# A background sum stepped at every fourth stop of a recurrence in both layers, instead of at every second stop in the first

## The chip, the cores and the metric

The kernel runs on one core of one Trainium2 chip. The metric is device time of one execution in microseconds (us). TensorE is PE in the profile (its weight loads are PEld), VectorE is DVE, ScalarE is ACT, GpSimd is POOL, and SP issues most of the DMAs.

## The reference, cut to what matters

Two transformer-like blocks, each of two layers, run one after the other on a sequence of 512 x 1024 in float32. The first block has four branches per layer, of which one (RWKV-7) is a recurrence over time. The second block scales and shifts its activations by vectors that depend on nothing but two small inputs and a large matrix:

```python
def first_block(x, ...):
    for l in range(2):
        h = x @ w_in[l]                      # 1024 x 10016
        # y_rwkv: a scan over 512 steps, 8 heads, state 64 x 64
        # y_mla, y_conv, y_mem: two attentions and a convolution
        merged = sum(sigmoid(h_merge[n] + b_gate[n]) * (y[n] @ w_o_branch[l][n]) for n in range(4))
        x = layer_norm(ALPHA * x + merged @ w_out[l])
    return x

def second_block(x, c, ctx, c_ctx, w_ada, ...):
    for i in range(2):
        mod_x = silu(c) @ w_ada[i] + b_ada[i]        # w_ada[i] is 1024 x 6144
        mod_c = silu(c_ctx) @ w_ada[i] + b_ada[i]
        hx = rms_norm(x) * (1 + sc1) + sh1           # pieces of mod_x
        ...                                          # attention, pooling, Fourier mix, feed-forward
```

`mod_x` and `mod_c` for `i = 0` do not depend on the first block, so their sums can be made at any time before the second block starts.

## The kernel before, in words

Every weight matrix is streamed from HBM in pieces of 512 KB. `wload` (lines 224 to 250) gets a piece into a tile `wst` by a DMA from SP, ACT rounds it into `wh`, DVE subtracts to get the rest `wl` (`split`, line 208), and `mm3` (line 203) makes each product with three matmuls. There are two buffers of `wst` and four of `wh` and of `wl` (`self.wb = (2, 4)`). A `wst` buffer is free again once `wl` is made.

The modulation sums are a generator, `ada(l)` (lines 1320 to 1347). It takes `w_ada` in 24 column blocks of 256 and each block in two halves of 512 rows. A half is one DMA of 512 KB into a `wst` tile of the same two buffers (line 1331); then DVE multiplies and adds its four row groups into `aacc`, once for `c` and once for `c_ctx`: eight DVE instructions per half, and only after the last of them is the buffer free. After both halves come two transposes into `atr` (line 1344) and a reduction into `adared` (line 1345). For `l = 0` the generator yields five times per block, 120 times in all. `tick2` (line 170) advances it by one yield, if there is one left.

The recurrence is `rwkv` (lines 522 to 869). It works by 64-step chunks: `prep` and `operands` make the operands of a head pair, `triangles` the 64 x 64 triangular matrices (through small DMAs `tri`, `BL`, `stk` of SP), `substitute` and `doubling` invert them, `chain` carries the state from chunk to chunk through short PE, DVE and ACT steps (`rbd`, `ubd`, `sbd`), and `close` normalises. Wherever these generators yield, `turns` calls `spot`: a stop. At a stop `drip` advances the filler of large matmuls (the merges of the three other branches, and gates), and `tick2` may advance the modulation sums. There are 248 stops per layer (5 of `prep`, 5 of `triangles`, 8, 12 of `doubling`, seven rounds of 29, and 15). `spots` is counted anew in each layer.

Before, `tick2` is called at each odd stop: 124 calls in the first layer, enough for all 120 yields, so the generator is exhausted there and the calls of the second layer do nothing. After the second layer's recurrence `while self.bg2: self.tick2()` (line 1297) would finish what is left. The sums of the second block's second layer (`ada(1)`) run later, in the feed-forward, and are not touched.

The order in which instructions stand on each engine is made when the kernel is built, by a scheduler that goes by priorities and by when it thinks an engine will be free; every engine then works through its own list in order. Weights have a higher priority than what stands around them (`high_priority` in `wload`).

Of the kernel before, what the change touches and what calls it, by code (L numbers as in the profile page):

```python
# [127 lines left out]
class K:  # L128
# [393 lines left out]
    def rwkv(self, l, st):  # L522
# [286 lines left out]
        spots = [0]  # L809

        def spot(w):

            self.drip(w)
            spots[0] += 1
            if spots[0] % 2:
                self.tick2()

        def turns(w, main, *side):

            for _ in main:  # L820
                spot(w)
                for t in side:
                    next(t, None)
            for t in side:
                for _ in t:
                    spot(w)
# [16 lines left out]
        for _ in prep(0):  # L843
            spot(0.5)
# [1174 lines left out]
```

## Time and profile before

| | |
|---|---|
| median of 3 runs | 3273.27 us (3270.59 to 3274.57) |
| the profiled execution | 3272.34 us |
| its span, first to last instruction | 3270.3 us |
| PE busy, share of the span | 3126.8 us, 96% |
| DVE busy | 2300.7 us, 70% |
| ACT busy | 1276.8 us, 39% |
| mean granted TensorE clock | 0.984 |

Times in the views are from the start of the span. The recurrence of the first layer lies at about 327 to 857 us, that of the second at 1239 to 1705 us, and the feed-forward of the second block's first layer at about 2080 to 2640 us. A clock of 1.00 in a view is 2.4 GHz throughout; the other level is 1.2 GHz.

### The profile page before, as it was taken

The page shows a single profiled execution, that of the slowest core. Times are in us where ns is not written, and L with a number is a line of the kernel's source. Part 1 is how long each engine was busy: PE and PEld are TensorE (multiplying, and loading weights), DVE is VectorE, ACT ScalarE, POOL GpSimd, SP SyncE. Part 2 cuts the span into 40 slices and gives each one's busy share as a digit, 9 for nine tenths or more (in the row PEclk, how much of TensorE's full clock was granted, in tenths as well). Part 3 has the DMA queues.
Part 4 walks back from the last instruction along what each step waited for, and adds up shares of the span by engine and source line. Part 5 has one row for each costly group of instructions (what it writes and reads, how often), then busy time and mean ns, then how long its engine had stood idle before and what let it go on. Part 6 is the DMA issues. An engine that isn't in the chain of part 4 may idle for free.

```text
span 3270.3 us, 44267 instructions
## 1 busy us (share of the span) xinstructions
PE 3126.8 (96%) x16694; PEld 2610.3 (80%) x16694; DVE 2300.7 (70%) x4916; ACT 1276.8 (39%) x2332; POOL 85.3 (3%) x176
## 2 busy tenths in 40 slices
PE   8999999899999999999999799989999999999999
PEld 7877777687898778888889776878888887688887
DVE  8978888888769886666658887875464468863342
ACT  4445333333344464444434556312121234732221
POOL 0001000000000000000000000000000000000000
PEclk9999999999999999999999899999999999999999
DMA  5322334334453223223234212344343232123332
GB/s 176 89 63 66 110 107 114 100 102 116 146 149 84 58 59 86 63 71 82 63 112 116 76 51 79 100 121 128 103 135 91 86 112 73 42 85 97 97 98 88
DMA packets 438661, 310.07 MB, mean 95 GB/s; under 512 B 69024, under 2 KB 430544, under 8 KB 438448
## 3 DMA queue, kind: packets, MB, share of 16 engines
q1 hardware_dynamic: 431392, 292.60, 31.0%
q0 software_dynamic: 7056, 14.65, 1.8%
q8 instruction: 132, 2.16, 0.3%
q14 instruction: 81, 0.66, 0.1%
HBM read 295.13 MB, written 7.34 MB: 92 GB/s over the span
## 4 chain that ended last, share of the span: by engine, by line
PE 49%; DVE 8%; DMA 3%; ACT 3%; issue 1%; SPq 0%; ACTq 0%; POOL 0%; DVEq 0%
PE ps_mm L197 40%; PE ps_o L197 2%; PE ps_tp L197 2%; DMA wst<-in_w_gate_up_dram 2%; DVE wl L186 2%; PE ps_aux L197 1%; PE ps_sc L197 1%; ACT wh L209 1%; DVE aacc L194 1%; DMA wst<-in_w_in_dram 1%; PE ps_mx L197 1%; PE ps_yb L197 1%; DVE n2t L194 0%; DVE z L186 0%; DMA wst<-in_w_ada_dram 0%
## 5 line engine op out<-in xcount | busy, mean ns | idle before, releaser
L209 ACT CAST wh<-wst 128x1024 fp32r<-128x1024 f32 (+3 forms) x453 | 458.5, 1013 | 1035.5 <-PE ps_mm L197 563.9
L186 DVE TENSOR_TENSOR wl<-wst,wh 128x1024 fp32r<-128x1024 f32 (+3 forms) x453 | 532.4, 1175 | 341.3 <-ACT wh L209 337.3
L197 PE MATMUL ps_mm<-xh,wh 128*128 128x512 f32 (+1 forms) x1200 | 499.7, 417 | 20.8 <-ACT wh L209 16.8
L197 PE MATMUL ps_mm<-xh,wl 128*128 128x512 f32 (+1 forms) x1200 | 482.2, 402 | 1.9 <-DVE wl L186 1.8
L197 PE MATMUL ps_mm<-xl,wh 128*128 128x512 f32 (+1 forms) x1200 | 482.4, 402 | 0.0
L197 PE MATMUL ps_mm<-h8h,wh 128*128 128x512 f32 (+1 forms) x928 | 360.6, 390 | 14.0 <-ACT wh L209 12.4
L197 PE MATMUL ps_mm<-h8h,wl 128*128 128x512 f32 (+1 forms) x928 | 357.2, 386 | 3.4 <-DVE wl L186 3.4
L197 PE MATMUL ps_mm<-h8l,wh 128*128 128x512 f32 (+1 forms) x928 | 358.8, 387 | 0.1
L197 PEld LDWEIGHTS ps_mm<-xh,wh 128*128 128x128 f32 (+1 forms) x1200 | 228.8, 191 | 65.6 <-ACT wh L209 20.4
L197 PEld LDWEIGHTS ps_mm<-xh,wl 128*128 128x128 f32 (+1 forms) x1200 | 227.5, 190 | 51.9 <-DVE wl L186 6.4
L194 DVE SCALAR_TENSOR_TENSOR aacc<-wst,silc,aacc 128x256 f32<-128x256 f32 x560 | 250.7, 477 | 19.7 <-DMA wst<-in_w_ada_dram 15.8
L197 PEld LDWEIGHTS ps_mm<-xl,wh 128*128 128x128 f32 (+1 forms) x1200 | 228.7, 191 | 37.7 <-issue 0.2
L197 PEld LDWEIGHTS ps_mm<-h8h,wl 128*128 128x128 f32 x928 | 176.3, 190 | 41.5 <-DVE wl L186 6.1
L197 PEld LDWEIGHTS ps_mm<-h8h,wh 128*128 128x128 f32 x928 | 176.6, 191 | 36.8 <-ACT wh L209 14.4
L197 PEld LDWEIGHTS ps_mm<-h8l,wh 128*128 128x128 f32 x928 | 176.8, 191 | 20.7 <-DVE h8l L194 0.4
L197 PE MATMUL ps_mm<-fh,wl 128*128 128x512 f32 (+1 forms) x528 | 186.8, 354 | 2.1 <-DVE wl L186 2.1
L197 PE MATMUL ps_mm<-fl,wh 128*128 128x512 f32 (+1 forms) x528 | 187.6, 355 | 0.0
L197 PE MATMUL ps_mm<-fh,wh 128*128 128x512 f32 (+1 forms) x528 | 187.3, 355 | 0.0
L194 DVE SCALAR_TENSOR_TENSOR ft<-ft,ps_mm 128x512 f32<-128x512 f32 (+1 forms) x134 | 76.6, 586 | 138.5 <-PE ps_mm L197 80.6
L194 DVE SCALAR_TENSOR_TENSOR cacc<-ch,vec,cacc 128x512 f32<-128x512 f32 x240 | 168.7, 746 | 2.3 <-ACT cacc L183 1.8
L197 PE MATMUL ps_mm<-hch,wl 128*128 128x256 f32 x448 | 126.7, 284 | 1.8 <-DVE wl L186 1.8
L197 PE MATMUL ps_mm<-hcl,wh 128*128 128x256 f32 x448 | 126.5, 284 | 0.7 <-DVE hcl L194 0.6
(549 smaller groups left out, 6413.9 us busy)
## 6 DMA issues: line engine op xcount, KB each, us to landing
wst<-in_w_in_dram SPq DMA_DIRECT2D x188, 512.0 KB, 3.9
wst<-in_w_ada_dram SPq DMA_DIRECT2D x96, 512.0 KB, 3.7
wst<-in_w_gate_up_dram SPq DMA_DIRECT2D x88, 512.0 KB, 4.0
wst<-in_w_out_dram SPq DMA_DIRECT2D x40, 512.0 KB, 3.5
wst<-in_w_down_dram SPq DMA_DIRECT2D x36, 512.0 KB, 3.5
wst<-in_w_o_branch_dram SPq DMA_DIRECT2D x32, 512.0 KB, 3.5
wst<-in_xattn_w_mem_kv_dram SPq DMA_DIRECT2D x16, 512.0 KB, 3.5
wst<-in_w_down_dram SPq DMA_DIRECT2D x20, 384.0 KB, 3.1
```

The lines of the kernel that those rows point to most:

```text
L186: return self.nc.vector.tensor_tensor(out=out, in0=a, in1=b, op=op)
L194: return self.nc.vector.scalar_tensor_tensor(out=out, in0=a, scalar=s, in1=b, op0=op0, op1=op1)
L197: self.nc.tensor.matmul(out, lhsT=l, rhs=r, start=start, stop=stop)
L209: self.nc.scalar.copy(out=h, in_=src)
```

## The change

The condition in `spot` is different, and nothing else:

```diff
             self.drip(w)
             spots[0] += 1
-            if spots[0] % 2:
+            if spots[0] % 4 == 1:
                 self.tick2()
```

Now 62 of the 248 stops of a layer advance the sums. The generator gets 62 of its 120 yields in the first layer and the other 58 in the second. In halves of `w_ada`, which are DMAs: before, 48 in the first layer; now 25 in the first and 23 in the second.

What stands on SP in the first layer, between the load of the fourth triangle (`BL<-tri_85`) and that of the fifth (`BL<-tri_84`). Before:

```order
L656 DMA BL<-tri_85 64x8x8
L1331 DMA wst<-in_w_ada_dram 128x4x256
L235 DMA wst<-in_w_in_dram 128x8x128 x2
L1331 DMA wst<-in_w_ada_dram 128x4x256
L695 DMA tri_87<-sub_3147 64x8x8
L698 DMA stk<-tri_87 32x4x32 x4
L235 DMA wst<-in_w_o_branch_dram 128x4x256
L235 DMA wst<-in_w_in_dram 128x4x256 x2
L1331 DMA wst<-in_w_ada_dram 128x4x256 x4
L235 DMA wst<-in_w_o_branch_dram 128x4x256
L654 DMA tri_84<-AB 64x4x64 x2
L656 DMA BL<-tri_84 64x8x8
```

And now, at the same place on SP:

```order
L656 DMA BL<-tri_85 64x8x8
L235 DMA wst<-in_w_in_dram 128x8x128 x2
L695 DMA tri_87<-sub_3147 64x8x8
L698 DMA stk<-tri_87 32x4x32 x4
L1331 DMA wst<-in_w_ada_dram 128x4x256
L235 DMA wst<-in_w_o_branch_dram 128x4x256
L235 DMA wst<-in_w_in_dram 128x4x256 x2
L1331 DMA wst<-in_w_ada_dram 128x4x256 x2
L235 DMA wst<-in_w_o_branch_dram 128x4x256
L654 DMA tri_84<-AB 64x4x64 x2
L235 DMA wst<-in_w_in_dram 128x4x256
L656 DMA BL<-tri_84 64x8x8
```

Six loads of `w_ada` stood here, four of them in a row; now there are three, at most two in a row. Six pieces of weights stood here before, and seven now.

The same in the second layer, from its first triangle (`BL<-tri_84`) to its second (`BL<-tri_85`). Before:

```order
L656 DMA BL<-tri_84 64x8x8
L235 DMA wst<-in_w_o_branch_dram 128x4x256
L235 DMA wst<-in_w_in_dram 128x4x256
L695 DMA tri_86<-sub_11633 64x8x8
L235 DMA wst<-in_w_in_dram 128x4x256
L698 DMA stk<-tri_86 32x4x32 x4
L235 DMA wst<-in_w_in_dram 128x8x128 x2
L654 DMA tri_85<-AB 64x4x64 x2
L235 DMA wst<-in_w_in_dram 128x8x128
L656 DMA BL<-tri_85 64x8x8
```

And now:

```order
L656 DMA BL<-tri_84 64x8x8
L1331 DMA wst<-in_w_ada_dram 128x4x256
L235 DMA wst<-in_w_o_branch_dram 128x4x256
L695 DMA tri_86<-sub_11344 64x8x8
L698 DMA stk<-tri_86 32x4x32 x4
L235 DMA wst<-in_w_in_dram 128x4x256 x2
L1331 DMA wst<-in_w_ada_dram 128x4x256
L235 DMA wst<-in_w_in_dram 128x8x128
L654 DMA tri_85<-AB 64x4x64 x2
L656 DMA BL<-tri_85 64x8x8
```

Two loads of `w_ada` stand here now, where there was none, each with weights before and behind it. Outside the two recurrences the lists of DVE and SP read alike before and after.

## Rows read from the trace of the kernel before

**Rows 1.** The page: the span in 40 slices of 82 us
```profile
DVE  8978888888769886666658887875464468863342
...
PEclk9999999999999999999999899999999999999999
```

**Rows 2.** Where the recurrences begin (wlal) and end (yf of each layer)
```profile
L194 DVE SCALAR_TENSOR_TENSOR wlal<-ps_mm,om,mx x2: 743/743/743, 326.2 to 1239.1; 128x511 f32<-128x511 f32 x2
...
L194 DVE SCALAR_TENSOR_TENSOR yf<-yc,g x4: 684/685/692, 510.1 to 856.9; 128x512 f32<-128x512 f32 x4
...
L194 DVE SCALAR_TENSOR_TENSOR yf<-yc,g x4: 648/650/692, 1406.1 to 1704.3; 128x512 f32<-128x512 f32 x4
```

**Rows 3.** Busy time by stretch: the two recurrences; the next-to-last figures are clock, DMA share
```profile
core 0: us, PE busy (x) PEld busy (x) DVE busy (x) ACT busy (x) POOL busy (x), PEclk, DMA share, GB/s
327.00:857.00 530.00, 487.75 (x2479) 399.79 (x2478) 449.27 (x1227) 192.96 (x416) 3.16 (x6) 0.95 0.38 110
1239.00:1705.00 466.00, 463.75 (x2503) 384.51 (x2502) 285.86 (x779) 191.65 (x416) 5.58 (x11) 1.00 0.28 74
```

**Rows 4.** What PE waited for, 327 to 857 us: us, times, longest
```profile
PE ps_mm L197 <- ACT wh L209: 16.8, 13, 4.0
PE ps_aux L197 <- ACT ubd L745: 5.6, 6, 3.4
PE ps_aux L197 <- ACT rbd L745: 5.1, 6, 3.0
PE ps_tp L197 <- DVE stk L732: 3.9, 3, 3.1
PE ps_tp L197 <- DVE X L186: 2.3, 1, 2.3
```

**Rows 5.** Instructions on wst, 327 to 857 us (ns min/median/max), and their waits
```profile
L194 DVE SCALAR_TENSOR_TENSOR aacc<-wst,silc,aacc x330: 433/476/487, 335.2 to 832.8; 128x256 f32<-128x256 f32 x165
L209 ACT CAST wh<-wst x60: 1033/1047/1057, 329.4 to 856.4; 128x1024 fp32r<-128x1024 f32 x60
L186 DVE TENSOR_TENSOR wl<-wst,wh x59: 1194/1224/1227, 330.5 to 854.3; 128x1024 fp32r<-128x1024 f32 x59
L1331 SPq DMA_DIRECT2D wst<-in_w_ada_dram x47: 367/368/597, 331.7 to 824.0; - x47
...
  PE ps_mm L197: 28.0, 7
...
  ACT wh L209: 62.0, 33
...
DMA to landing us min/median/max: 3.3/3.7/5.3
```

**Rows 6.** The same, 1239 to 1705 us
```profile
  PE ps_mm L197: 105.6, 38
...
  ACT wh L209: 4.3, 3
```

**Rows 7.** The feed-forward and a stretch of full DVE: columns as in rows 3
```profile
2300.00:2600.00 300.00, 298.10 (x1691) 259.20 (x1690) 150.05 (x266) 59.02 (x88) 0.00 (x0) 1.00 0.36 108
...
1000.00:1050.00 50.00, 49.95 (x248) 41.40 (x247) 49.23 (x83) 24.37 (x56) 0.55 (x1) 1.00 0.31 85
```

**Rows 8.** Loads of w_ada, 2300 to 2600 us: ns min/median/max, first and last
```profile
L1331 SPq DMA_DIRECT2D wst<-in_w_ada_dram x24: 367/368/368, 2330.5 to 2529.6; - x24
```

**Rows 9.** Two gaps of PE in order of time: 504 to 512 and 591 to 594 us
```profile
504.15 1.05 ACT L209 CAST wh<-wst 128x1024 fp32r<-128x1024 f32 x1 [4.86 <-DMA wst<-in_w_o_branch_dram]
...
512.09 0.79 PE L197 MATMUL ps_mm<-xh,wh 128*128 128x512 f32 x1 [3.98 <-ACT wh L209]
...
593.17 0.47 DVE L194 SCALAR_TENSOR_TENSOR aacc<-wst,silc,aacc 128x256 f32<-128x256 f32 x1
593.57 0.21 DVE L744 COPY rbd<-ps_yb 64x64 f32<-64x64 f32 x1
...
594.12 0.49 PE L197 MATMUL ps_aux<-rbd,AB 128*128 128x128 f32 x2 [3.02 <-ACT rbd L745]
```

## The prediction, made before the changed kernel had run

> **What bounds the kernel now.** I read first the busy shares. PE is busy 96% of the span by the table above. DVE by slices of 82 us [rows 1] is at 7 or 8 tenths between 330 and 860 us (fifth to eleventh slice), and at 5 or 6 tenths between 1240 and 1700 us (sixteenth to twenty-first). The dips of the clock are hardly readable there, since a slice is long; they show below.
>
> Then I found the two recurrences by their first and last instructions [rows 2]: 326.2 to 857.6 us in the first layer (856.9 plus 0.7 for the last `yf`), 1239.1 to 1705.0 us in the second. They do the same work, and one is 531 us and the other 466 us long. The reader is to see in the two stretches side by side [rows 3] that PE has 2479 and 2503 records in them (some records are missing from a trace), but is idle for 42 us of 530 in the first and for 2 us of 466 in the second; and that the same matmuls are busy for 488 us in the first and 464 us in the second, where the granted clock is 0.95 against 1.00. So the first layer loses 65 us: 40 to gaps of PE, 24 to the clock that falls to 1.2 GHz in and behind the gaps. What the first layer has and the second has not is the modulation sums: DVE is busy 449 us there and 286 us here, 163 us more.
>
> Third I read what PE waits for in the first recurrence [rows 4]. Two kinds come out at the same size: 16.8 us for `wh`, rounded weights that are late, and 5.6 + 5.1 + 3.9 + 2.3 = 16.9 us for links of the chain of small steps (`ubd`, `rbd`, `stk`, `X`). One gap of each kind is shown in order of time [rows 9]: at 508 us ACT had waited 4.86 us for a piece's DMA and PE then 3.98 us for the next; at 591 us the DVE copy `rbd` stood behind the sums and PE waited 3.02 us.
>
> Fourth the tile `wst` [rows 5, 6]. In the first layer ACT waits 62 us in 33 of its 60 casts for the piece to land, and only 7 times for PE to free a buffer: the weights run late. In the second it waits 105.6 us, 38 times, for PE, and 4.3 us for landings: the weights are ahead, and PE sets the pace.
>
> **The change part by part.** No instruction is added or removed. All that moves is 23 of the 48 halves of `w_ada`, from the first recurrence to the second: their DMAs on SP, their multiply-adds, transposes and reductions on DVE. Outside the recurrences the lists are the same, so the sum has two terms, one for each recurrence.
>
> *DVE.* The sums cost 163 us of DVE in one layer [rows 3]. Moving 23/48 takes 78 us out of the first and puts them into the second: 449 - 78 = 371 us and 286 + 78 = 364 us. Against the 464 us that PE needs in a layer at full clock, that is 80% and 78%, where it was 97% and 62%. At 97% any lateness of DVE stays for a long time; at 80% it has some 95 us to catch up.
>
> *The two buffers of `wst`.* In 530 us two buffers give 1060 us, shared by 59 pieces of weights and 47 halves of `w_ada` [rows 5]: 10.0 us for each. A piece of weights needs at least 3.7 us to land, 1.05 us for the cast and 1.22 us for `wl`: 6.0 us, 354 us for 59. If the buffers are always taken, the halves hold (1060 - 354)/47 = 15.0 us each. With 24 halves in a layer and the same hold: 354 + 24 x 15.0 = 714 us of the 932 us that two buffers give in 466 us, 77%. So the weights can run ahead again, through four `wh` buffers, as in [rows 6]. Even one buffer alone would carry the weights, 354 of 466 us.
>
> *The first layer's gain.* If all its loss goes, 65 us. If the loss is in proportion to the halves, 65 x 23/48 = 31 us.
>
> *The second layer's loss.* At the least nothing, at the most in proportion, 65 x 23/48 = 31 us, unless something new starts there (a rival below).
>
> So the sum lies between -65 and 0 us. The nearest rows are these. In the feed-forward 24 halves of `w_ada` went through the same two buffers in 300 us, denser than 24 in 466 us, and PE was busy 298.1 us of 300 at clock 1.00 [rows 7, 8]; but a half there has mostly four multiply-adds, and there is no chain. At 1000 us DVE was busy 49.2 us of 50 and PE 49.95 [rows 7]: a full DVE alone does not stop PE where it feeds nothing urgent. Both rows are near no loss at all: 0.6% of 932 us is 6 us, a gain of 59. A loss that goes with the square of the number of halves would leave a quarter in each layer, 32 us in both, a gain of 33. I take 17 us left in both together, nearer to the rows than to the square, for the chain that these rows lack: -48 us. The profiled execution took 3272.3 us; 3272.3 - 48 = 3224, and with the median 1 us above that execution, 3225 us.
>
> At what the gaps cost I weigh a rule of the Trainium skill. The row: the work of PE took 24 us more at clock 0.95 than at 1.00 [rows 3]. The page "TensorE: Matmul & The Clock Gate" (HAM oscillation) puts the cost at the time at the low clock times one half; a mean of 0.95 is 10% of 530 us at the low level, so 26.5 us, an estimate by that page. The trace nearly agrees. [...] By the row that is 24/40, or 0.6 us for each us of gap; by the page, 26.5/40, or 0.66. The 17 us left include it.
>
> **The rivals.**
>
> *The loss only moves.* Each half stops PE by the same 65/48 = 1.35 us wherever it runs. Then 3273 us. For it: within the first recurrence PE's gaps of the second kind [rows 9] need only a few sums ahead of one link. Against it: the feed-forward's 24 halves cost under 2 us together [rows 7, 8], not 32. [...]
>
> *Every link of the chain still meets a sum.* What delays a link would then be that some sum stands before it in DVE's list, not how many. The chain's share of the first layer's gaps is 16.9 us, with the clock 16.9 x 1.6 = 27 us; this would now come in both layers, and the weights' share, also 16.8 x 1.6 = 27, split between them. The rest of the loss (65 - 54 = 11) likewise stays. So 27 us more than before: slower, 3300 us. It decides if the second recurrence's gaps on `rbd`, `ubd`, `stk` and `X` come to 17 us or more. For it: at 591 us a few multiply-adds and a `wl` were enough. Against: the same copies stood behind `wl`, `pr` and `mg` in the second layer before, and PE had 2 us of gaps [rows 3]; DVE now has 95 us of slack per layer.
>
> *Halves hold their buffer longer.* Two parts of a half lie one advance apart, which is now four stops and not two. 248 stops in 466 us are 1.9 us each; if the order on DVE followed the stops strictly, a half would hold 3.8 us longer, 15.0 + 3.8: 354 + 24 x 18.8 = 805 of 932 us, 86%. This is still not full; it would cost perhaps half of the gain, 3250 us.
>
> **How the numbers follow.** The forecast, most of the loss gone, has 0.77; it reaches from 3207 (all of it gone) to 3245 us. The long hold or a loss like the square with some more has 0.11, 3245 to 3266. The loss only moves: 0.06, 3267 to 3280. Every link meets a sum: 0.06, 3285 to 3310. The forecast's own range is 3207 to 3245; that leaves out somewhat more than 2 in 10, so I give 3206 to 3258. A measurement of this kernel can tell about 0.2%, 6.5 us, from no change. Faster takes the first two cases, 0.88; the same 0.06; slower 0.06.
>
> **What would show it.** The profile after should have both recurrences at 466 to 480 us; clock 0.98 or more in each; DVE busy near 370 us in each; PE idle under 10 us in each; ACT waiting mostly for PE and not for landings before `wh` in both; and `adared` 12 times in each layer. I am wrong if the first recurrence stays above 500 us (then neither the buffers nor DVE's load were the reason), if the second goes above 490 us, or if there is a gap between the recurrences, since the thirteenth block's `aacc` stays open over that stretch.

## The result

| | before | after |
|---|---|---|
| median | 3273.92 us (3270.59 to 3275.33, 4 runs) | 3224.48 us (3223.6 to 3226.89, 4 runs) |
| ratio | | 0.9855, 95% interval 0.984 to 0.9871 |
| the profiled execution, its span | 3272.34 us, 3270.3 us | 3226.89 us, 3224.8 us |
| first recurrence, from `wlal` to the last `yf` | 531.4 us | 470.8 us |
| second recurrence | 465.9 us | 475.0 us |

The change made the kernel faster by 49 us in the medians and by 45.4 us in the two profiled executions. The busy shares of the page of after, in 40 slices of 81 us, answer to [rows 1]:

```profile
DVE  8978787887789777877878786874554378853332
...
PEclk9999999999999999999999999999999999999999
```

DVE is at 7 or 8 tenths in both recurrences now. Where they begin and end in the trace of after, as in [rows 2]:

```profile
L194 DVE SCALAR_TENSOR_TENSOR wlal<-ps_mm,om,mx x2: 742/742/743, 325.3 to 1181.1; 128x511 f32<-128x511 f32 x2
...
L194 DVE SCALAR_TENSOR_TENSOR yf<-yc,g x4: 684/686/691, 492.3 to 795.4; 128x512 f32<-128x512 f32 x4
...
L194 DVE SCALAR_TENSOR_TENSOR yf<-yc,g x4: 682/684/691, 1346.7 to 1655.4; 128x512 f32<-128x512 f32 x4
```

With 0.7 us for the last `yf` the first recurrence lost 60.6 us and the second gained 9.1. What lies before the first is 0.9 us shorter, what lies between them 385.0 us instead of 381.5, and what comes behind 1568.7 instead of 1565.3. The sum, -60.6 + 9.1 - 0.9 + 3.5 + 3.4 = -45.5 us, is the difference of the spans. The stretch between is not quite the same work: the first of the second layer's 23 halves, its load and its eight multiply-adds, stands ahead of `wlal` and so lies in it:

```profile
L1331 SPq DMA_DIRECT2D wst<-in_w_ada_dram x1: 368/368/368, 1154.3 to 1154.3; - x1
```

Behind the second recurrence the lists of DVE, ACT and SP are the same. The two recurrences by engine, with the columns of [rows 3]:

```profile
core 0: us, PE busy (x) PEld busy (x) DVE busy (x) ACT busy (x) POOL busy (x), PEclk, DMA share, GB/s
326.00:796.00 470.00, 463.78 (x2482) 383.71 (x2482) 368.17 (x1008) 191.22 (x416) 3.10 (x6) 1.00 0.36 98
1181.00:1656.00 475.00, 467.71 (x2502) 387.31 (x2501) 364.10 (x990) 191.29 (x416) 5.44 (x11) 0.99 0.35 97
```

DVE is busy 368 and 364 us. In the first stretch PE's gaps fell from 42 us to 6.2, and its busy time from 488 us to 464, with the clock back at 1.00. In the second the gaps rose from 2.3 us to 7.3 and the busy time from 464 to 468. The longest waits of PE in the first stretch, which answer to [rows 4]:

```profile
PE ps_aux L197 <- ACT rbd L745: 1.4, 3, 0.5
PE ps_aux L197 <- ACT ubd L745: 1.2, 4, 0.4
PE ps_mm L197 <- ACT tg L183: 1.0, 2, 0.8
PE ps_mm L197 <- ACT wh L209: 0.7, 1, 0.7
```

Both kinds of gap went together: late weights from 16.8 us to 0.7, links of the chain from 16.9 us to under 3. No wait is over 0.8 us. In the second stretch:

```profile
PE ps_tp L197 <- DVE rq_t L186: 1.4, 1, 1.4
PE ps_aux L197 <- ACT rbd L745: 1.1, 2, 0.6
PE ps_tp L197 <- DVE rq_a L191: 1.0, 1, 1.0
PE ps_aux L197 <- ACT ubd L745: 0.8, 3, 0.3
```

What the casts waited for in the trace of after, first stretch and then second, answers to [rows 5] and [rows 6] (first the idle time before instructions on `wst` by what ended it, then who waited):

```profile
  PE ps_mm L197: 72.4, 25
...
  ACT wh L209: 28.5, 17
```

```profile
  PE ps_mm L197: 74.8, 23
...
  ACT wh L209: 49.7, 15
```

In the first stretch ACT waits 28.5 us for landings, where it was 62.0, and 72.4 us for PE, where it was 28.0. The weights run ahead more often, but not always: 17 of the 60 casts there still wait for a landing, where it was 33, and 15 in the second stretch, where it was 3.

### The profile page after: what moved, and what is told of

The parts are those of the page before. It is cut to its first block, busy times and chain, and to the rows that moved or that the text cites. A ratio compares the mean times of both kernels' runs of the same rounds, so it can differ in the third digit from the quotient of the medians.

```text
span 3224.8 us, 44259 instructions
## 1 busy us (share of the span) xinstructions
PE 3112.1 (97%) x16694; PEld 2601.2 (81%) x16694; DVE 2299.8 (71%) x4916; ACT 1273.7 (39%) x2332; POOL 84.9 (3%) x176
## 4 chain that ended last, share of the span: by engine, by line
PE 48%; DVE 10%; ACT 4%; DMA 4%; issue 1%; ACTq 0%; POOL 0%; DVEq 0%; SPq 0%
PE ps_mm L197 39%; DVE wl L186 2%; PE ps_o L197 2%; DMA wst<-in_w_gate_up_dram 2%; PE ps_tp L197 2%; DMA wst<-in_w_in_dram 1%; ACT wh L209 1%; PE ps_sc L197 1%; DVE aacc L194 1%; PE ps_aux L197 1%; PE ps_mx L197 1%; DVE n2t L194 1%; PE ps_yb L197 0%; DVE z L186 0%; DVE h8l L194 0%
```

## The experiments

Lengths of the recurrences below are taken as in the table above. The time that each is set against is that of the kernel before on the same chip.

**The loads left out.** Before's cadence, with the sums on data that are already there:

```diff
-                st = self.wpool.tile([P, 4, 256], F32, name="wst", tag="wst", bufs=self.wb[0])
-                src = self.a["w_ada_2"][l]...
-                nc.sync.dma_start(out=st, in_=src...)
+                if l == 0:
+                    st = self.xh.bitcast(F32)[:, 4 * half:4 * half + 4, 0:256]
+                else:
+                    ...
```

> Before's cadence (every second stop, first layer), but the sums of the second block's first layer read 48 x 4 columns groups of a tile that is always there (xh) instead of loads of w_ada: the 48 DMAs are left out (so the modulation values are not those of the reference), all DVE instructions stay. Two theories of why the first recurrence lost 65 us. Theory D, the load of DVE (449 us of the 464 us that PE needs): the loss stays, first recurrence 515 to 531 us, time 3258 to 3273 us. Theory S, the two wst buffers that the halves share with the weights: the first recurrence falls to 466 to 475 us, ACT waits under 15 us for landings, time 3207 to 3220 us. If both are needed, in between, about 3240 us.

3233.21 us against 3270.76, ratio 0.9885 (0.9865 to 0.9906). The first recurrence took 493.6 us, the second 466.2. The first, by engine:

```profile
326.00:819.00 493.00, 473.36 (x2495) 390.61 (x2493) 442.26 (x1221) 191.59 (x416) 3.24 (x6) 0.99 0.26 71
```

What two of PE's waits came to in it, and then how long ACT's casts waited for a landing:

```profile
PE ps_mm L197 <- DVE wl L186: 3.4, 1, 3.4
PE ps_mm L197 <- ACT wh L209: 0.7, 1, 0.7
```

```profile
  ACT wh L209: 17.7, 12
```

DVE is as full as before, 442 us, and still 38 of the 65 us are gone. DVE's load alone does not make the loss: theory D fell, as far as it claimed all. But 28 us stay without any load of `w_ada`, so the buffers alone don't make it either. What is left of the gaps is no longer late `wh` (0.7 us, 16.8 before): it is spread over many results, most of them of DVE, and the longest single wait is for one `wl`. The relief is not pure: DVE, too, no longer waits for halves to land (8.5 us before).

**Half of the sums left out.** Before's cadence, all loads:

```diff
-                    for k in range(4):
+                    for k in ((0, 3) if l == 0 else range(4)):
```

> Before's cadence and all 48 loads of w_ada in the first layer, but of each half only two of four row groups are multiplied and added (the other half of the sum is left out): 192 of 384 multiply-adds go. Theory D: DVE falls from 449 to about 449 - 192 x 0.41 = 370 us, as in the changed kernel, so the first recurrence takes 470 to 480 us and the time is 3213 to 3228 us. Theory S: 47 halves still hold a buffer each, for perhaps 1.6 us less than 15.0: 354 + 47 x 13.4 = 984 us of 932, so the first recurrence stays at 495 to 520 us, 3240 to 3262 us.

3225.95 us against 3270.76, ratio 0.9862 (0.9842 to 0.9883). The first recurrence took 484.6 us. By engine, and then how long ACT's casts waited for a landing in it:

```profile
327.00:811.00 484.00, 468.05 (x2484) 387.40 (x2483) 380.21 (x1040) 190.81 (x416) 3.10 (x6) 0.99 0.42 120
```

```profile
  ACT wh L209: 54.4, 26
```

And of PE's waits the longest in sum, and that for late weights:

```profile
PE ps_aux L197 <- ACT rbd L745: 3.3, 5, 1.2
PE ps_mm L197 <- ACT wh L209: 1.3, 2, 0.7
```

The weights are nearly as late as before (54.4 us of waits for landings, 62.0 before), yet the first recurrence lost only 19 us, and PE waited 1.3 us for `wh`, where it was 16.8. With DVE at 380 us a piece that lands late is made up for. Theory S fell too, as far as it claimed all: its least time was 495 us. This relief is not pure either, since a half with four multiply-adds frees its buffer sooner; the landings say that little came of it.

**Both at once.** The two edits above together:

```diff
+                if l == 0:
+                    st = self.xh.bitcast(F32)[:, 4 * half:4 * half + 4, 0:256]
...
-                    for k in range(4):
+                    for k in ((0, 3) if l == 0 else range(4)):
```

> Before's cadence with both reliefs at once: the sums of the second block's first layer read a resident tile (no loads of w_ada there) and only two of four row groups are summed (both left out of the computation). If the first recurrence's loss is DVE's load and the two shared buffers and nothing else, it now takes 466 to 474 us (it was 493.6 us without the loads and 484.6 us with half of the sums), and the time is 3207 to 3216 us. If a third thing delays PE (the stops themselves, the transposes and reductions), the first recurrence stays at 480 us or more and the time at 3220 us or more.

3203.47 us against 3275.18, ratio 0.9777 (0.9761 to 0.9793). The first recurrence took 467.4 us, the second 465.7:

```profile
326.00:792.00 466.00, 461.55 (x2480) 383.38 (x2479) 373.04 (x1035) 190.66 (x416) 3.25 (x6) 1.00 0.27 72
```

Almost nothing is left: against the second recurrence before (465.9 us), the stops, the transposes, the reductions and the other half of the sums cost under 2 us together. The first recurrence's 65 us fall by 38 without the loads, by 47 without half of the sums, and by 64 without both. The two parts are not added (38 + 47 is 85): 28 us are there with the full DVE alone, 19 us with all the loads alone, and the other 18 us only where both meet, late weights and a DVE that can't catch up.

**Every third stop in both layers.**

```diff
-            if spots[0] % 2:
+            if spots[0] % 3 == 1:
```

> Advances at every third stop in both layers: 33 halves in the first, 15 in the second. Both theories have the loss bend with the load: first recurrence DVE 449 - 163 x 15/48 = 398 us (86% of 464), buffers 354 + 33 x 15.0 = 849 of 932 us (91%): a loss of 10 to 25 us there and 3 us in the second, 3225 to 3243 us. If the loss were in proportion above a threshold at the changed kernel's density (25 halves), the first would lose 4 + 61 x 8/23 = 25 us and the time would be 3240 us.

3239.21 us against 3270.76, ratio 0.9898 (0.9882 to 0.9913). The first recurrence took 493.0 us, the second 467.6. The loads of `w_ada` in the first layer and in the second, and then the two recurrences by engine:

```profile
L1331 SPq DMA_DIRECT2D wst<-in_w_ada_dram x34: 367/368/452, 300.6 to 796.6; - x34
...
L1331 SPq DMA_DIRECT2D wst<-in_w_ada_dram x14: 367/368/390, 1207.6 to 1408.3; - x14
```

```profile
328.00:820.00 492.00, 474.91 (x2483) 391.45 (x2482) 399.69 (x1091) 191.53 (x416) 3.31 (x6) 0.98 0.37 103
1202.00:1669.00 467.00, 463.81 (x2500) 384.02 (x2499) 333.37 (x911) 191.29 (x416) 5.60 (x11) 1.00 0.33 89
```

So it is 34 halves and 14, not the 33 and 15 of the expectation. With 34 DVE is worked out at 449 - 163 x 14/48 = 401 us, and it was 400. The loss of 27 us is a little above the 10 to 25 expected. The other reckoning, a loss in proportion beyond 25 halves, gave 25 us and 3240 us (28 us with 34 halves), and comes nearest.

**All in the second layer.**

```diff
-            if spots[0] % 2:
+            if l == 1 and spots[0] % 2:
```

> All 48 halves at every second stop of the second layer's recurrence, none in the first. If the loss belongs to the density of the halves (theories D and S alike), it moves over whole: first recurrence 466 us, second 525 to 535 us, time 3265 to 3280 us. If the first layer's recurrence has something of its own that stops it (its place behind the other branches, its weights), the second takes 466 to 490 us and the time is 3205 to 3235 us.

3272.31 us against 3270.76, ratio 1.0007 (0.9994 to 1.002). The first recurrence took 464.8 us, the second 528.0:

```profile
325.00:789.00 464.00, 462.29 (x2482) 383.54 (x2481) 284.86 (x780) 191.62 (x416) 3.25 (x6) 1.00 0.27 72
1175.00:1703.00 528.00, 486.30 (x2501) 397.82 (x2500) 450.00 (x1226) 192.92 (x416) 5.97 (x12) 0.96 0.40 112
```

The loss moved over whole, with its 450 us of DVE and its clock of 0.96. So it takes nothing that only the first layer has.

With the kernel before and after this gives the length of a recurrence by the halves of `w_ada` in its layer (one of them can stand just ahead of it): 0 halves 464.8 to 466.2 us; 14 halves 467.6; 23 halves 475.0; 25 halves 470.8; 34 halves 493.0; 48 halves 528.0 and 531.4. Up to 25 the cost is 0.1 to 0.4 us a half; from 25 to 34 each costs 2.5 us, and from 34 to 48 2.5 to 2.7 us.

**A slower start of the other sums.** In the feed-forward of the second block's first layer the sums of its second layer (`ada(1)`) begin with column blocks for both `c` and `c_ctx`, eight multiply-adds in a half. The changed kernel, and:

```diff
                     self.split(ah(f), al(f), t)
                     self.tick2()
-                    self.tick2()
+                    if f0 + f >= 8:
+                        self.tick2()
```

> The changed kernel, and besides the sums of the second block's second layer advance once instead of twice per stream in the first eight columns of the feed-forward, and twice from then on (the same 72 advances). In the changed kernel PE is idle 17 us between 2030 and 2250 us and the clock is at 0.93 to 0.97 from 2050 to 2200 us, some 25 us lost where the halves of w_ada carry eight multiply-adds each and DVE is at 80%. If this is the same loss by density, half the density there takes away half to three quarters of it: 3206 to 3214 us. If it is the feed-forward's own start (weights late behind the modulation of the activations), nothing changes: 3222 to 3228 us. If the later columns now stop, slower than 3228 us.

3210.47 us (3207.03 to 3221.13) against 3275.18, ratio 0.9804 (0.9782 to 0.9825). That is below the changed kernel's ratio, 0.9855 (0.984 to 0.9871); the intervals do not touch. The start of the feed-forward and the rest of it, and what PE waited for most at the start, in the changed kernel:

```profile
2030.00:2250.00 220.00, 202.98 (x1109) 174.43 (x1108) 147.66 (x310) 46.98 (x74) 0.00 (x0) 0.96 0.38 115
2250.00:2600.00 350.00, 348.26 (x1936) 301.97 (x1935) 171.50 (x295) 72.95 (x107) 0.00 (x0) 1.00 0.35 105
```

```profile
PE ps_mm L197 <- ACT wh L209: 13.0, 6, 3.7
```

and in this one:

```profile
2030.00:2250.00 220.00, 217.25 (x1254) 189.43 (x1253) 126.77 (x254) 48.42 (x76) 0.00 (x0) 1.00 0.32 96
2250.00:2600.00 350.00, 343.82 (x1940) 297.65 (x1939) 208.06 (x389) 80.35 (x116) 0.00 (x0) 1.00 0.40 122
```

In the first 220 us PE is idle 2.8 us where it was 17.0, with 14 loads of `w_ada` instead of 23; no wait of PE for `wh` is left there, the clock stays at 1.00, and 1254 matmuls are done instead of 1109. Later, where the sums stand closer now, PE is idle 6.2 us where it was 1.7.

## Why the prediction was right

*The terms.* DVE was to be busy 371 and 364 us; it was 368 and 364. The first recurrence was to lose most of its 65 us, and lost 60.6. Of the loss 17 us was to be left in both; 4.9 us (470.8 - 465.9) and 9.1 us are left, 14.0 together. The clock, PE's idle time and the 12 `adared` in each layer are as the signs had them. The time was forecast at 3225 us and is 3224.48. That the match is so close is partly luck. The profiled execution was to take 3224 us and took 3226.89, and the median lies 2.4 us below it, not 1 us above. And some 7 us more lie outside the recurrences, which the sum had at nothing. Of these, 3.5 us are in the stretch between, which now holds one half: with a half in it, this stretch takes 384.6 to 386.1 us in the three traces that have one, and without it 380.3 to 382.0 us in the five others. So "outside the recurrences the lists are the same" was not quite so. The other 3.4 us are in the stretch behind, whose lists are the same (1568.7 against 1565.3). In the runs of the experiments that leave these lists alone it takes 1560.6 to 1568.7 us, so it may be the spread of single executions; that is not shown.

*The cause.* The prediction named two, DVE at 97% of PE's time and the two buffers, and did not say which decides. The runs show that it is the two together: either relief alone takes 38 or 47 of the 65 us, both 64; and either alone ends PE's waits for late `wh`, from 16.8 us to 0.7 or 1.3. Halving the density relieves both at once, and so is worth nearly as much as taking both away.

*The buffers' step was only half right.* "The weights can run ahead again" holds for a part of the casts: ACT still waits 28.5 and 49.7 us for landings, and the condition "mostly for PE and not for landings in both" was met (72.4 and 74.8 us for PE), in the second by less. What changed is that a late piece no longer stops PE: 0.7 us of gaps in the first stretch.

*The rivals.* "The loss only moves" fell: it moves only when the density moves with it, as in the run with all halves in the second layer. "Every link of the chain still meets a sum" fell: it was to decide from 17 us of gaps on `rbd`, `ubd`, `stk` and `X` in the second recurrence, and that has 7.3 us of gaps of all kinds. The longer hold is there, but is not dear: from the issue of its load to the end of its last multiply-add a half took about 13.0 us on average before (not the 15.0 worked out), and 14.9 and 16.4 us in the two layers after, taking loads and multiply-adds in the order in which they start. That is 372 us for 25 halves and 378 us for 23, which with 354 us for the weights is 77% of two buffers in either recurrence, as forecast. What it costs can't be seen apart: it is within the 9 us.

*The rows it rested on.* The loss does not grow with the square of the halves, which would have left 32 us, but bends, and stays near nothing up to 25, as the two rows of the feed-forward and of the full DVE suggested. At 34 halves the loss of 27 us is not far below the square, 65 x (34/48)^2 = 33; at 25 it is 4.9 us where the square gives 18, and at 14 it is 1.7 us where the square gives 5.5. The row of the feed-forward was the easy part of it, though: at its start, where a half has eight multiply-adds, the trace of before has PE idle for 14 of 150 us:

```profile
2100.00:2250.00 150.00, 135.60 (x751) 116.52 (x750) 114.76 (x244) 34.42 (x57) 0.00 (x0) 0.98 0.43 128
```

So the feed-forward as a whole did not speak against a loss by density; the last experiment found it there. The clock followed the gaps: in the first recurrence 24 us came back, as [rows 3] had priced it, and in the second PE's busy time rose by 4 us.

*Open.* Why the second recurrence loses 9.1 us with 23 halves and the first 4.9 with 25. Most of the difference is the clock: PE's gaps are 7.3 and 6.2 us, but its busy time is 4 us longer in the second. The low clock comes at one place there, and in the first recurrence nowhere. At that place, at 1451 us, the trace of after shows two gaps close together on the doubling's transposes, behind the steps of `close` (a reduction and the root):

```profile
1450.56 0.22 DVE L186 TENSOR_TENSOR stk<-stk,ps_tp 128x64 f32<-128x64 f32 x1
1450.70 0.68 DVE L794 TENSOR_REDUCE gvar<-s 128x8 f32<-128x512 f32 x1
...
1451.30 0.23 DVE L732 STREAM_TRANSPOSE stk<-stk 128x64 f32<-128x64 f32 x1
...
1451.68 0.60 PE L197 MATMUL ps_tp<-stk,AD 128*128 128x32 f32 x4 [1.03 <-DVE rq_a L191]
...
1454.85 0.39 PE L197 MATMUL ps_tp<-stk,AO 128*128 128x32 f32 x1 [1.42 <-DVE rq_t L186]
```

The granted clock from there on, with the columns of [rows 3]:

```profile
1450.00:1452.00 2.00, 0.97 (x8) 0.77 (x8) 1.94 (x9) 1.17 (x2) 0.00 (x0) 1.00 0.28 52
1452.00:1454.00 2.00, 1.36 (x11) 1.14 (x10) 1.94 (x11) 0.00 (x0) 0.00 (x0) 0.83 0.70 210
1454.00:1456.00 2.00, 1.15 (x5) 1.18 (x6) 1.92 (x7) 1.04 (x1) 0.00 (x0) 0.50 0.01 4
...
1458.00:1460.00 2.00, 2.00 (x6) 1.61 (x5) 2.00 (x8) 0.38 (x2) 0.00 (x0) 0.50 0.65 225
1460.00:1462.00 2.00, 2.00 (x10) 1.56 (x10) 0.79 (x2) 0.20 (x1) 0.00 (x0) 0.97 0.13 23
```

It is at 1.2 GHz from about 1453 to 1460 us. Why these two gaps fell together in the second layer and not in the first is not shown.

## What to carry to other kernels

In this kernel background work that was spread over a stretch cost little until the engine and the buffers that it shares came near the time of the engine that sets the pace: little with DVE busy for 368 of PE's 464 us, 27 us at 400, 65 us at 449. Read such a share against that engine's busy time, not against the stretch, which the stalls have lengthened. Two resources that are both nearly full can make a larger loss together than each by itself (65 us against 28 and 19), so that relieving either pays more than its part. When such work can wait, spread it over all stretches with room, and look for the next place where it stands too close: here the start of the feed-forward, worth another 14 us between the two medians (each beside its own runs of the kernel before, which differ by 1.3 us).

## What was not expected

Without any load of `w_ada`, DVE's 442 us still cost the first recurrence 28 us; and with weights late by 54.4 us in all, it lost only 19 us when DVE had room. That the four buffers behind the cast cover late landings as long as DVE turns them over at once would explain the second; it is not shown, since no run changed their number.
